# Moving half of the modulation's partial sums to GpSimd, and the substitution of the small diagonal blocks to VectorE

## The chip, the cores and the metric

The kernel runs on one core of one Trainium2 chip. The metric is the device time of one launch in microseconds. The times are those of repeated launches of the same program; the profile is one further execution, recorded by the hardware profiler.

## The reference

One decoder block for 256 tokens of width 2048, in float32. A vector `c` gives six modulation vectors of 2048 elements each; the normalised input is scaled and shifted by the first two, one wide projection feeds a recurrent branch (RWKV-7) and a windowed attention branch, both are gated, merged and added to `x`, and a squared-ReLU MLP follows.

```python
c_act = jax.nn.silu(c)
mod = c_act @ w_ada[l] + b_ada[l]                      # 2048 x 12288
sh1, sc1, gt1, sh2, sc2, gt2 = [m[:, None, :] for m in jnp.split(mod, 6, axis=-1)]
h = rms_norm(x, norm1_gain[l]) * (1.0 + sc1) + sh1
p = h @ w_in[l] + b_in[l]
...
y_rwkv = rwkv7_branch(p_rwkv, ...)                     # a scan over 256 tokens, 16 heads of 64
y_attn = sliding_window_sink_attention(q, k, v, attn_sinks[l])
merged = g_rwkv * (y_rwkv @ w_branch_rwkv[l]) + g_attn * (y_attn @ w_branch_attn[l])
x = x + gt1 * (merged @ w_out[l])
h = rms_norm(x, norm2_gain[l]) * (1.0 + sc2) + sh2
x = x + gt2 * (jnp.square(jax.nn.relu(h @ w_up[l])) @ w_down[l])
return rms_norm(x, final_gain)
```

## The kernel before

**Weights.** Every large product goes through `feed` or `rows_product`. Both take the weight in tiles of 128 x 1024 floats (512 KB): a DMA from the SyncE queue into a tile `raw`, a cast on ScalarE to a rounded copy `whi` (L278), a subtraction on VectorE that leaves the remainder `wlo` (L279), and then 24 matmuls of 256 columns (or 12 of 512) on TensorE (L301, L323). `whi` and `wlo` have four buffers each, `raw` has seven.

**The modulation** is a product of one row with a 2048 x 12288 matrix. It is cut in segments of 2048 columns (`seg`, six of them) and those in pieces: `ada_tile` (L141) loads 128 x 2 x 512 floats (512 KB) into a buffer of the same seven `raw` buffers, and `ada_dve` (L211) multiplies each half by one column of `cact` and adds it into `acc` (L221 for the first half of the first piece, L223 for the others). Eight pieces make 512 columns; `ada_sum` (L186) then sums `acc` over the partitions with four matmuls against a column of ones (L190) and adds the bias on VectorE (L192, L194). The first 512 columns of segments 0 and 1 are done by TensorE (`ada_pe`).

**Order.** Three lists of generators, `bg` (modulation), `att` (attention) and `rw` (recurrence), stand beside the weight stream. After each weight tile `pulse(0.5)` advances every list by its rate; for `bg` the rate counts double, so that `rate["bg"]` is the number of steps per weight tile. What is written in this order is then laid out by a scheduler, engine by engine; each engine and the SyncE queue run their own list strictly in order.

**Stages.** The projection runs in four parts of four blocks of the contraction (`SL`), 16 weight tiles each. While parts 0, 1 and 2 run, `modulated(1)` to `modulated(3)` (L377) compute the 512 columns of segments 1 and 0 that the next part's input needs, 16 pieces each at 1.5 steps per tile; `finish(bg)` closes each part. After the parts come the rest of the projection (gates, keys; tiles of 256 columns x 4 blocks), the attention branch's product, the recurrent branch's product, the output product and the MLP. Segments 2, 4 and 3 (`ada_vec`, L227; 32 pieces each) run under these at `RATE_BG` 0.9, then 0.3 and 0.4 steps per tile; segment 5 runs under the MLP at 0.2.

**The recurrence** runs in two passes of four of the eight head pairs. Each pass has `prep` (which clears one column of `eP` on GpSimd at L510 before VectorE's scan at L529 reads it), `inverse16` (L613), `levels` and `chains`. `inverse16` loads the 128 diagonal 16 x 16 blocks, one a partition, from a DRAM scratch tile (L616), inverts them by 15 steps of a multiply and an add on GpSimd (L624, L626; 15 to 64 elements a partition), copies the transposed blocks (L628), and sends both through another DRAM tile back into `dds` (L627, L629, L634), which `levels` reads on TensorE.

## Time and profile before

| | us |
|---|---|
| time, median of 3 runs | 1545.87 (1545.2 to 1548.84) |
| time of the profiled execution | 1552.83 |
| span in its profile | 1551.1 |
| TensorE busy | 1488.3 |
| VectorE busy | 1099.2 |
| ScalarE busy | 721.6 |
| GpSimd busy | 40.5 |

The span is the profiled execution from its first to its last instruction; 1.7 us of its own time lie around it, and its own time lies 7.0 us above the median of the runs. Matmuls overlap in the pipeline and their ends are modelled, so TensorE's busy share is no measure of how close it is to its peak. Waits are put down to the releaser that came last by the profile. A row of a group of instructions gives the line, the engine, the operation, the tiles written and read, their shape and the count, then the busy time in us and the mean of one in ns, and behind the second bar the idle time before them and what ended it.

### The profile page before, as it was taken

The numbers are of one execution on the slowest core, as the hardware profiler recorded it, in microseconds if no ns is written. First come the engines' busy times: TensorE is split into PE (matmuls) and PEld (weight loads), VectorE is DVE, ScalarE is ACT, GpSimd is POOL, SyncE is SP. The second block draws the span as 40 slices with busy tenths as digits, with TensorE's granted clock in tenths as the row PEclk, the third lists the DMA queues.
The fourth block names the chain that finished last, engine by engine and source line by source line (L and its number), as shares of the span: only waits on it lengthen the run. The fifth ranks groups of instructions, "written<-read, shape, count | busy, mean of one in ns | idle before, by whom it ended". The sixth has DMA issues, their size and how long they took to land.

```text
span 1551.1 us, 30141 instructions
## 1 busy us (share of the span) xinstructions
PE 1488.3 (96%) x12122; PEld 1366.5 (88%) x12122; DVE 1099.2 (71%) x1784; ACT 721.6 (47%) x1107; POOL 40.5 (3%) x97
## 2 busy tenths in 40 slices
PE   5899999999999989999899999999999999999997
PEld 2898998999898989899789998989899898989985
DVE  1979979978689947768679765666666665555576
ACT  3354377656364424444456544434344443444443
POOL 2000000030000030000000000000000000000000
PEclk9899999999999999999999999999999999999998
DMA  9999977779898768878775777777776776666662
GB/s 331 334 317 318 353 236 230 245 191 327 244 288 287 233 188 287 266 252 301 247 234 167 237 226 237 217 224 231 222 232 213 233 229 204 189 190 190 196 185 82
DMA packets 297100, 372.80 MB, mean 240 GB/s; under 512 B 40912, under 2 KB 198384, under 8 KB 296320
## 3 DMA queue, kind: packets, MB, share of 16 engines
q1 hardware_dynamic: 296448, 370.72, 75.3%
q8 instruction: 95, 1.56, 0.4%
q0 software_dynamic: 512, 0.15, 0.1%
q14 instruction: 45, 0.37, 0.1%
HBM read 357.96 MB, written 12.86 MB: 239 GB/s over the span
## 4 chain that ended last, share of the span: by engine, by line
PE 77%; DMA 8%; DVE 8%; issue 2%; POOL 2%; ACT 2%; SPq 1%; DVEq 0%; POOLq 0%; ACTq 0%
PE mm L301 34%; PE mm L323 14%; PE ax L323 14%; PE ax L301 7%; DMA ada<-in_w_ada_dram 5%; DVE acc L223 2%; DVE wlo L279 2%; DMA raw<-in_w_in_dram 1%; PE ax L190 1%; POOL p L626 1%; PE ax L688 1%; POOL rs L624 1%; PE ax L482 1%; PE ax L571 1%; ACT whi L278 1%
## 5 line engine op out<-in xcount | busy, mean ns | idle before, releaser
L278 ACT CAST whi<-raw 128x1024 fp32r<-128x1024 f32 x458 | 478.5, 1048 | 605.8 <-PE ax L323 219.7
L279 DVE TENSOR_TENSOR wlo<-raw,whi 128x1024 fp32r<-128x1024 f32 x458 | 557.2, 1220 | 241.0 <-ACT whi L278 237.1
L301 PE MATMUL mm<-h,whi 128*128 128x256 f32 (+1 forms) x3296 | 433.4, 282 | 3.4 <-ACT whi L278 3.4
L301 PEld LDWEIGHTS mm<-h,whi 128*128 128x128 f32 (+1 forms) x3296 | 403.7, 188 | 10.2 <-ACT whi L278 3.8
L223 DVE SCALAR_TENSOR_TENSOR acc<-ada,cact,acc 128x512 f32<-128x512 f32 x330 | 247.1, 749 | 88.4 <-DMA ada<-in_w_ada_dram 84.0
L301 PE MATMUL mm<-h,wlo 128*128 128x256 f32 (+1 forms) x1648 | 232.7, 282 | 0.0
L301 PEld LDWEIGHTS mm<-h,wlo 128*128 128x128 f32 (+1 forms) x1648 | 210.8, 190 | 0.4 <-DVE wlo L279 0.2
L323 PE MATMUL mm<-whi,u 128*128 128x512 f32 x512 | 137.2, 390 | 0.0
L323 PE MATMUL ax<-whi,u 128*128 128x512 f32 x512 | 136.9, 389 | 0.0
L301 PE MATMUL ax<-h,whi 128*128 128x256 f32 x768 | 106.8, 287 | 9.3 <-DVE p L974 4.7
L323 PEld LDWEIGHTS ax<-whi,u 128*128 128x128 f32 x512 | 96.1, 188 | 20.0
L323 PEld LDWEIGHTS mm<-whi,u 128*128 128x128 f32 x512 | 95.5, 188 | 19.3
L301 PEld LDWEIGHTS ax<-h,whi 128*128 128x128 f32 x768 | 98.0, 194 | 11.7 <-ACT whi L278 5.1
L323 PE MATMUL mm<-wlo,u 128*128 128x512 f32 x256 | 78.8, 389 | 0.0
L323 PE MATMUL ax<-wlo,u 128*128 128x512 f32 x256 | 78.8, 389 | 0.0
L301 PE MATMUL ax<-h,wlo 128*128 128x256 f32 x384 | 57.8, 283 | 0.0
L323 PEld LDWEIGHTS mm<-wlo,u 128*128 128x128 f32 x256 | 48.1, 188 | 10.0
L323 PEld LDWEIGHTS ax<-wlo,u 128*128 128x128 f32 x256 | 48.1, 188 | 10.0
L301 PEld LDWEIGHTS ax<-h,wlo 128*128 128x128 f32 x384 | 51.3, 193 | 0.0
L301 PE MATMUL mm<-a,whi 128*128 128x256 f32 x256 | 37.9, 299 | 0.0
L323 PE MATMUL mm<-whi,m 128*128 128x512 f32 x128 | 36.3, 401 | 0.0
L323 PE MATMUL ax<-whi,m 128*128 128x512 f32 x128 | 36.1, 403 | 0.0
(345 smaller groups left out, 1493.2 us busy)
## 6 DMA issues: line engine op xcount, KB each, us to landing
ada<-in_w_ada_dram SPq DMA_DIRECT2D x192, 512.0 KB, 5.9
raw<-in_w_up_dram SPq DMA_DIRECT2D x128, 512.0 KB, 4.1
raw<-in_w_down_dram SPq DMA_DIRECT2D x128, 512.0 KB, 4.1
raw<-in_w_in_dram SPq DMA_DIRECT2D x72, 512.0 KB, 6.0
raw<-in_w_in_dram SPq DMA_DIRECT2D x128, 256.0 KB, 5.7
raw<-in_w_out_dram SPq DMA_DIRECT2D x32, 512.0 KB, 5.3
raw<-in_w_branch_attn_dram SPq DMA_DIRECT2D x16, 512.0 KB, 5.9
raw<-in_w_branch_rwkv_dram SPq DMA_DIRECT2D x16, 512.0 KB, 5.2
```

The lines of the kernel that those rows point to most:

```text
L190: TE.matmul(ps[:, j:j + 1], lhsT=acc[:, j * P:(j + 1) * P], rhs=ones[:, 0:1], start=True, stop=True)
L223: V.scalar_tensor_tensor(o, in0=t[:, a, :], scalar=ck, in1=o, op0=ALU.mult, op1=ALU.add)
L278: S.copy(hi[:], raw[:])
L279: V.tensor_tensor(lo[:], raw[:], hi[:].bitcast(F32), op=ALU.subtract)
L301: TE.matmul(ps[0:m, j * tw:(j + 1) * tw], lhsT=wt[:, kk, o:o + m], rhs=xx(k), start=(k == begin and xx is xh and wt is hi and j == 0), sto ...
L323: TE.matmul(pss[tb][:], lhsT=uu(k)[:, sl], rhs=wt[:, kk, :], start=(first and k == 0), stop=(final and k == kblocks - 1))
L482: TE.matmul(out[hs, :], lhsT=src[hs, chunk(c)], rhs=ident[hs, hs], start=True, stop=True)
L571: TE.matmul(pT[hs, o:o + P], lhsT=src[hs, chunk(c)], rhs=ar[hs, i, c].rearrange("p a b -> p (a b)"), start=True, stop=True)
L624: G.tensor_tensor(t_, a16[:, s, m:16].unsqueeze(2).broadcast_to([P, n, m]), x16[:, 0, s:s + 1, 0:m].broadcast_to([P, n, m]), op=ALU.mult)
L626: G.tensor_tensor(x16[:, 0, m:16, 0:m], x16[:, 0, m:16, 0:m], t_, op=ALU.add)
L688: TE.matmul(ps[hs, j, i, part, :], lhsT=lhs(j, i, hs), rhs=rhs(j, i, hs), start=(first and j == 0 and i == 0), stop=True, skip_group_check ...
```

## The change

Four edits. `ada_pool` is new: it does a piece on GpSimd, with one multiplication of the whole 128 x 1024 tile by two columns of `cact` (in place), and two additions of 512 columns into its own `acc` (one for the first piece); it has one empty step before its `ada_sum`. `turns` runs several generators a step each in turn. `modulated(1)` to `modulated(3)` and `ada_vec` now give segment 0 (or every second group of 512 columns) to `ada_pool` and segment 1 (or the other groups) to `ada_dve`. `inverse16` moves its 30 operations and the copy from GpSimd to VectorE and takes one of the empty steps behind it to before it. `RATE_BG[0]` goes from 0.9 to 1.0.

```diff
-RATE_BG = (0.9, 0.3, 0.4, 0.2)
+RATE_BG = (1.0, 0.3, 0.4, 0.2)
...
+    def ada_pool(seg, k0, n, dst, gain):
+
+        acc = wp.tile([P, 512], F32, tag="acc", bufs=NACC, name=nm("acc"))
+        o = acc[:, 0:n * P]
+        m = 8 // n
+        for q in range(2 * n):
+            t = ada_tile(seg, k0, n, q)
+            G.tensor_tensor(t[:], t[:], cact[:, m * q:m * q + m].unsqueeze(2).broadcast_to([P, m, n * P]), op=ALU.mult)
+            if q == 0:
+                G.tensor_tensor(o, t[:, 0, :], t[:, 1, :], op=ALU.add)
+            else:
+                for a in range(m):
+                    G.tensor_tensor(o, t[:, a, :], o, op=ALU.add)
+            yield
+        yield
+        ada_sum(acc, n, dst, k0, seg, gain)
+
+    def turns(gens):
...
     def ada_vec(seg, dst, gain=None):
-        for k0 in range(0, KC, 4):
-            yield from ada_dve(seg, k0, 4, dst, gain)
+        for k0 in range(0, KC, 8):
+            yield from turns([ada_dve(seg, k0, 4, dst, gain), ada_pool(seg, k0 + 4, 4, dst, gain)])
...
+            yield from turns([ada_pool(0, k0, n, sh1, None), ada_dve(1, k0, n, sc1, colC[:, 96:96 + KC])])
...
+        yield
         for s in range(15):
...
-            G.tensor_tensor(t_, a16[:, s, m:16].unsqueeze(2).broadcast_to([P, n, m]),
+            V.tensor_tensor(t_, a16[:, s, m:16].unsqueeze(2).broadcast_to([P, n, m]),
...
-            G.tensor_tensor(x16[:, 0, m:16, 0:m], x16[:, 0, m:16, 0:m], t_, op=ALU.add)
+            V.tensor_tensor(x16[:, 0, m:16, 0:m], x16[:, 0, m:16, 0:m], t_, op=ALU.add)
...
-        G.tensor_copy(x16[:, 1], x16[:, 0].rearrange("p a b -> p b a"))
+        V.tensor_copy(x16[:, 1], x16[:, 0].rearrange("p a b -> p b a"))
...
-        for _ in range(5):
+        for _ in range(4):
             yield
```

How the instructions stand now (line numbers of the kernel changed: L308 is the subtraction that was L279, L1006 the eviction that was L974).

**Part 1 of the projection, VectorE before.** `acc_1173` collects a piece of the modulation, `p_44` a projection's sum.

```order
L223 SCALAR_TENSOR_TENSOR acc_1173<-ada_1250,cact,acc_1173 128x512
L974 TENSOR_TENSOR p_44_235<-ax_1178,p_44_235 128x512
L223 SCALAR_TENSOR_TENSOR acc_1173<-ada_1250,cact,acc_1173 128x512
L974 TENSOR_TENSOR p_44_235<-ax_1179,p_44_235 128x512
L279 TENSOR_TENSOR wlo_1262<-raw_1258,whi_1261 128x1024
L223 SCALAR_TENSOR_TENSOR acc_1173<-ada_1289,cact,acc_1173 128x512 x2
L279 TENSOR_TENSOR wlo_1297<-raw_1293,whi_1296 128x1024
L223 SCALAR_TENSOR_TENSOR acc_1173<-ada_1324,cact,acc_1173 128x512 x2
L223 SCALAR_TENSOR_TENSOR acc_1173<-ada_1328,cact,acc_1173 128x512
```

The same place on VectorE now:

```order
L223 SCALAR_TENSOR_TENSOR acc_1021<-ada_1255,cact,acc_1021 128x512
L1006 TENSOR_TENSOR p_44_235<-ax_1182,p_44_235 128x512
L223 SCALAR_TENSOR_TENSOR acc_1021<-ada_1255,cact,acc_1021 128x512
L1006 TENSOR_TENSOR p_44_235<-ax_1183,p_44_235 128x512
L308 TENSOR_TENSOR wlo_1267<-raw_1263,whi_1266 128x1024
L308 TENSOR_TENSOR wlo_1303<-raw_1299,whi_1302 128x1024
L223 SCALAR_TENSOR_TENSOR acc_1021<-ada_1330,cact,acc_1021 128x512 x2
```

And on GpSimd in the same part, where no instruction stood before:

```order
L234 TENSOR_TENSOR ada_986<-ada_986,cact 128x1024
L236 TENSOR_TENSOR acc_985<-ada_986 128x512
L234 TENSOR_TENSOR ada_1026<-ada_1026,cact 128x1024
L239 TENSOR_TENSOR acc_985<-ada_1026,acc_985 128x512 x2
L234 TENSOR_TENSOR ada_1097<-ada_1097,cact 128x1024
L239 TENSOR_TENSOR acc_985<-ada_1097,acc_985 128x512 x2
```

Between two weight tiles VectorE has half as many pieces of the modulation; GpSimd has eight multiplications and fifteen additions in each of three parts.

**GpSimd from the first heads on, before.** `kd` holds the attention's keys, `p_...` are the `eP` tiles that `prep` clears, `rs` and `p_522` belong to `inverse16`.

```order
L910 COPY kd<-a_50_249 64x256 x4
L510 MEMSET p_358_2634 128x4
L510 MEMSET p_367_2651 128x4
L510 MEMSET p_440_3229 128x4
L510 MEMSET p_444_3241 128x4
```

And now:

```order
L942 COPY kd<-a_50_249 64x256 x4
L541 MEMSET p_358_2655 128x4
L234 TENSOR_TENSOR ada_3056<-ada_3056,cact 128x1024
L236 TENSOR_TENSOR acc_3055<-ada_3056 128x512
L541 MEMSET p_367_2672 128x4
L234 TENSOR_TENSOR ada_3251<-ada_3251,cact 128x1024
L239 TENSOR_TENSOR acc_3055<-ada_3251,acc_3055 128x512 x2
L234 TENSOR_TENSOR ada_3417<-ada_3417,cact 128x1024
```

The small clears that VectorE's scans wait for now stand behind pieces of the modulation; the `inverse16` rows that followed them are gone from GpSimd.

**The second `inverse16`, now on VectorE.** `rs_7031` and `p_914` are its product and its blocks, `lg_7028` the loaded blocks.

```order
L308 TENSOR_TENSOR wlo_7149<-raw_7146,whi_7148 128x1024
L656 TENSOR_TENSOR rs_7031<-lg_7028,p_914_7030 128x15
L308 TENSOR_TENSOR wlo_7187<-raw_7184,whi_7186 128x1024
L658 TENSOR_TENSOR p_914_7030<-p_914_7030,rs_7031 128x15
L656 TENSOR_TENSOR rs_7031<-lg_7028,p_914_7030 128x28
L658 TENSOR_TENSOR p_914_7030<-p_914_7030,rs_7031 128x14x2
L656 TENSOR_TENSOR rs_7031<-lg_7028,p_914_7030 128x39
L658 TENSOR_TENSOR p_914_7030<-p_914_7030,rs_7031 128x13x3
```

These rows stood on GpSimd without others between them; now they stand among the subtractions for the weight stream, which follow in the same queue.

## Rows read from the trace of the kernel before

**Rows 1.** The page: busy time and share of the span of each engine.

```profile
PE 1488.3 (96%) x12122; PEld 1366.5 (88%) x12122; DVE 1099.2 (71%) x1784; ACT 721.6 (47%) x1107; POOL 40.5 (3%) x97
```

**Rows 2.** Busy time by stage; the first row names the columns.

```profile
core 0: us, PE busy (x) PEld busy (x) DVE busy (x) ACT busy (x) POOL busy (x), PEclk, DMA share, GB/s
38.00:189.00 151.00, 137.02 (x1102) 134.51 (x1101) 134.52 (x181) 62.02 (x77) 0.00 (x0) 0.95 0.99 331
247.00:655.00 408.00, 391.07 (x4750) 364.63 (x4749) 322.47 (x744) 198.81 (x415) 28.98 (x68) 0.98 0.82 255
857.00:1551.00 694.00, 683.46 (x4385) 623.08 (x4383) 434.40 (x485) 297.52 (x334) 0.00 (x0) 0.99 0.67 208
```

**Rows 3.** VectorE's groups between 38 and 189 us.

```profile
L223 DVE SCALAR_TENSOR_TENSOR acc<-ada,cact,acc 128x512 f32<-128x512 f32 x90 | 67.3, 749 | 1.7
L279 DVE TENSOR_TENSOR wlo<-raw,whi 128x1024 fp32r<-128x1024 f32 x45 | 54.4, 1220 | 5.3 <-ACT whi L278 5.1 <-DMA raw<-in_w_in_dram 0.2
L390 DVE TENSOR_TENSOR h<-ar,h 128x256 fp32r<-128x256 f32 x8 | 3.1, 422 | 0.9 <-ACT h L389 0.8
L221 DVE TENSOR_SCALAR acc<-ada,cact 128x512 f32<-128x512 f32 x6 | 2.9, 483 | 0.1
```

**Rows 4.** Who waited for whom, 38 to 189 us: us in total, times, longest.

```profile
ACT whi L278 <- DMA raw<-in_w_in_dram: 46.2, 23, 4.7
ACT whi L278 <- DVE acc L223: 13.9, 4, 5.5
```

**Rows 5.** Who waited for whom over the span, SyncE's DMA queue.

```profile
SPq L290 <- DVE wlo L279: 278.9, 158, 6.9
```

**Rows 6.** GpSimd's operations, 321 to 339 us; last, a clear at the start.

```profile
L626 POOL TENSOR_TENSOR p<-p,rs 128x15 f32<-128x15 f32 x2 | 0.5, 227 | 0.2
L624 POOL TENSOR_TENSOR rs<-lg,p 128x15 f32<-128x15 f32 x2 | 0.4, 216 | 42.7 <-DMA lg<-scr 42.6
L626 POOL TENSOR_TENSOR p<-p,rs 128x64 f32<-128x64 f32 x1 | 0.3, 318 | 0.1
L624 POOL TENSOR_TENSOR rs<-lg,p 128x64 f32<-128x64 f32 x1 | 0.3, 295 | 0.1
...
L608 POOL MEMSET a<- 128x520 f32 x1 | 0.6, 551 | 0.0
```

**Rows 7.** GpSimd and VectorE in order of time: start us, us, what; at 551.7 us.

```profile
551.97 1.15 POOL L626 TENSOR_TENSOR p<-p,rs 128x48 f32<-128x48 f32 x1
...
551.68 1.29 DVE L279 TENSOR_TENSOR wlo<-raw,whi 128x1024 fp32r<-128x1024 f32 x1
```

**Rows 8.** The same view at 337.8 us.

```profile
337.81 0.64 POOL L628 COPY p<-p 128x256 f32<-128x256 f32 x1
337.88 1.65 DVE L279 TENSOR_TENSOR wlo<-raw,whi 128x1024 fp32r<-128x1024 f32 x1 [1.82 <-ACT whi L278]
```

**Rows 9.** VectorE's groups between 247 and 655 us.

```profile
L223 DVE SCALAR_TENSOR_TENSOR acc<-ada,cact,acc 128x512 f32<-128x512 f32 x148 | 110.7, 748 | 41.1 <-DMA ada<-in_w_ada_dram 39.5
L279 DVE TENSOR_TENSOR wlo<-raw,whi 128x1024 fp32r<-128x1024 f32 x87 | 106.4, 1229 | 20.3 <-ACT whi L278 19.3 <-PE mm L301 0.8
L221 DVE TENSOR_SCALAR acc<-ada,cact 128x512 f32<-128x512 f32 x9 | 4.3, 483 | 2.2 <-DMA ada<-in_w_ada_dram 2.2
L360 DVE TENSOR_TENSOR rd<-rd 128x4 f32<-128x4 f32 x22 | 3.2, 156 | 0.0
```

**Rows 10.** The chain that ended last, 247 to 655 us: shares by engine and line.

```profile
by line: PE mm L301 21.9%; DMA ada<-in_w_ada_dram 14.0%; issue 6.5%; DVE wlo L279 6.3%; DVE acc L223 6.2%; POOL p L626 3.7%; PE ax L688 3.6%; POOL rs L624 3.1%; PE ax L571 2.4%; PE ax L482 2.3%; DMA raw<-in_w_in_dram 2.0%; DMA lw<-in_rwkv_w
```

**Rows 11.** In order of time: the starts of both substitutions, and VectorE then.

```profile
321.45 0.21 POOL L624 TENSOR_TENSOR rs<-lg,p 128x15 f32<-128x15 f32 x1 [42.63 <-DMA lg<-scr]
...
322.65 0.16 DVE L840 TENSOR_SCALAR m<-m 128x4 f32<-128x4 f32 x1
...
548.48 0.58 POOL L624 TENSOR_TENSOR rs<-lg,p 128x15 f32<-128x15 f32 x1 [42.68 <-DMA lg<-scr]
...
548.90 1.24 DVE L279 TENSOR_TENSOR wlo<-raw,whi 128x1024 fp32r<-128x1024 f32 x1
```

**Rows 12.** Who waited for whom between 857 and 1551 us.

```profile
ACT whi L278 <- PE ax L323: 184.2, 114, 2.6
```

**Rows 13.** The chain over the span in order of time: 384 matmuls of 256 columns.

```profile
1046.79 45.23 PE mm L301 x384
```

More of the change, by code (lines that the diff above doesn't have):

```diff
@@ L225, in ada_dve @@
         ada_sum(acc, n, dst, k0, seg, gain)
+    def ada_pool(seg, k0, n, dst, gain):
[14 more added lines that the diff above has]
+    def turns(gens):
+        gens = list(gens)
+        while gens:
+            for g in list(gens):
+                try:
+                    next(g)
+                except StopIteration:
+                    gens.remove(g)
+                    continue
+                yield
     def ada_vec(seg, dst, gain=None):
-        for k0 in range(0, KC, 4):
-            yield from ada_dve(seg, k0, 4, dst, gain)
+        for k0 in range(0, KC, 8):
+            yield from turns([ada_dve(seg, k0, 4, dst, gain), ada_pool(seg, k0 + 4, 4, dst, gain)])
     def drain(g):
@@ L378, in modulated @@
         k0, n = sum(SL[:part]), SL[part]
-        gemv = ada_pe if part == 0 else ada_dve
-        for seg in (1, 0):
-            yield from gemv(seg, k0, n, *((sc1, colC[:, 96:96 + KC]) if seg else (sh1, None)))
+        if part == 0:
+            for seg in (1, 0):
+                yield from ada_pe(seg, k0, n, *((sc1, colC[:, 96:96 + KC]) if seg else (sh1, None)))
+        else:
+            yield from turns([ada_pool(0, k0, n, sh1, None), ada_dve(1, k0, n, sc1, colC[:, 96:96 + KC])])
         for k in range(k0, k0 + n):
@@ L620, in inverse16 @@
         yield
+        yield
         for s in range(15):
```

## The prediction, made before the changed kernel was run

> **What bounds the kernel now.** I read the page's busy shares first: TensorE is busy 96% of the span and VectorE 71% [rows 1]. An average over stages says little, so the busy time by stage comes next [rows 2]. It shows three kinds of time. From 857 us on, the MLP, TensorE is busy 683 of 694 us and VectorE 434, and ScalarE's cast waits for TensorE to give buffers back, 184.2 us on one of its two lines alone [rows 12]. What VectorE or GpSimd do there is hidden: each weight tile takes 24 matmuls of 45.23/384 = 118 ns, 2.83 us [rows 13], against 1.2 us of subtraction. I call this stage C. From 38 to 189 us (stage A: the three projection parts that have the modulation in the background) VectorE is busy 134.5 of 151 us, 89%, and the DMA engines are busy 0.99 of the time at 331 GB/s [rows 2]; the cast waits for weights 46.2 us and for VectorE 13.9 us [rows 4], and the SyncE queue waits for VectorE before it can refill a buffer [rows 5]. So VectorE and the transfers bound stage A together. From 247 to 655 us (stage B: recurrence, attention and both branch products) VectorE is busy 322 of 408 us, the DMA engines 0.82 [rows 2], and the chain of work there is mixed: TensorE, 14% of waiting for pieces of the modulation to land, and 3.7% + 3.1% of GpSimd's substitution, 28 us [rows 10].
>
> **What leaves VectorE.** A piece costs it two operations of 0.75 us [rows 3], 1.5 us. In stage A half of 48 pieces go: 33.7 us of L223 and 1.5 us of L221, so VectorE's own work falls from 134.5 to 99 us. In stage B there were (148 + 9)/2 = 78 pieces [rows 9]. The weight tiles there number about 88; at 1.0 instead of 0.9 steps a tile, and with two empty steps in each 34, they now carry 88 x 32/34 = 83 pieces, 41 on either engine. That takes 37 x 1.5 = 56 us from VectorE.
>
> **What GpSimd pays for a piece.** No row has a GpSimd operation of that size, so I bound it. Two points of the substitution give a slope: the multiply goes from 216 ns at 15 elements to 295 at 64, 1.6 ns an element; the add from 227 to 318, 1.9 ns [rows 6]. At 1024 elements the multiply is then 0.22 + 1009 x 0.0016 = 1.8 us, and the add of 512 is 0.23 + 497 x 0.0019 = 1.15 us. Eight pieces (8 multiplies, 15 adds) take 14.5 + 17.3 = 32 us on GpSimd, where VectorE needs 12. The low end is the clear, which reads nothing: 551 ns for 520 elements, 1.06 ns each [rows 6], which gives 8 x 1.1 + 15 x 0.54 = 17 us. I take 32, since it comes from the same operation with two inputs.
>
> The Trainium skill, "GPSIMD Engine Reference", section "Performance versus the Vector engine", gives 4497 ns for an add of 2048 floats; as an estimate, half and a quarter of that make 8 x 2.25 + 15 x 1.12 = 35 us for eight pieces. No run here shows that size yet.
>
> **Whether that work lies beside VectorE's.** This decides the case. Two rows show that the two engines hold each other up. An add of 48 elements on GpSimd that started inside a subtraction of VectorE (551.68, 1.29 us) took 1.15 us instead of 0.3 and ended 0.15 us after it [rows 7]: GpSimd waited for VectorE's end. And a subtraction that started 0.07 us after a GpSimd copy of 0.64 us took 1.65 us instead of 1.22 [rows 8]: VectorE waited 0.43 us, until 0.14 us before the copy's end. The rows have only short GpSimd operations; I assume that a long one holds VectorE off in the same way, for its length less 0.14 us. Eight pieces then hold VectorE's operations with two SBUF inputs (L223, L279, L390) off for 32 - 23 x 0.14 = 29 us at most.
>
> What the Trainium skill says speaks against the change: "SBUF — State Buffer", section "SBUF: two separate sides", has the port pair that VectorE and GpSimd share as an exclusive lock, taken by whichever starts first and held for the whole instruction, also against a VectorE operation with two SBUF inputs. Rows 7 and 8 agree for operations up to 0.64 us; by this rule the next paragraph's sum holds, and if the 0.43 us seen were the most that one operation can block, the first rival's sum would.
>
> **Stage A.** VectorE's own work 99 us, GpSimd's hold 3 x 29 = 87 us. If the two simply exclude each other, that is 186 us, plus the 16 us that VectorE had idle at the joints of the parts, 202; if GpSimd also runs under the evictions and the joints, what is left is the work that excludes each other: 54.4 + 33.7 + 3.1 + 87 = 178 us. Against 151 us now this is +27 to +51; I take +40. With GpSimd's low end (17 - 3 = 14 us for eight pieces) it is 91 + 42 = 133 us, below the 151 that the transfers need anyway: 0. The transfers leave nothing to gain here: DMA share is 0.99.
>
> **Stage B.** VectorE's own work is 322 - 56 + 62 substitution operations. These I price between its smallest operations, 0.156 us [rows 9], and 0.2 us: 10 to 12 us. That makes 277 us. GpSimd holds 41/8 x 29 = 149 us. VectorE's two-input work (106 of subtractions, 61 of pieces, some 65 of small operations) fills about 230 of 408 us, 57%, so I expect 57% of 149, 85 us, of blocked time; the ends are half of that and all of it, 42 and 149. VectorE goes from 322 to 362 (319 to 426). Off this come half of the 41 us that it waited for pieces to land [rows 9], 21 us, which GpSimd now waits out, and the substitution's 28 us on the chain [rows 10] less its 11 on VectorE, 17 us. Sum: +40 - 21 - 17 = +2, ends -41 and +66. Added waits: the scan on VectorE waits for a clear on GpSimd, which now stands behind pieces, and the subtractions stand behind the scan; eight clears at up to one piece (1.8 + 2.3 = 4.1 us), of which TensorE's lead of up to four tiles hides most: 0 to +33, I take +8. `ada_sum`'s matmuls now wait for GpSimd's sum in TensorE's queue; the empty step gives it one tile: 0 to +10, I take +5. VectorE may also wait for the substitution's blocks to land; they landed at 321.4 and 548.5 us, and VectorE stood at the new place at about 322.6 and just before 548.9 [rows 11]: nothing. Stage B: +15, from -40 to +75.
>
> **Stage C and the rest.** 16 pieces of segment 5 leave VectorE, which waited for TensorE there anyway: 0. If GpSimd's holds came in a row they would be 4 us against a lead of four tiles, 11 us: still 0. Between 655 and 857 us few pieces are left: 0.
>
> **Sum.** +40 + 15 = +55 us on the profiled execution's own time, 1552.8, which gives 1608. That execution lies 7.0 us above the median of the runs, so I state 1601 and round to 1600.
>
> **The rivals.**
> *The blocking is short, and VectorE is relieved* (faster). If a GpSimd operation blocks VectorE by no more than the 0.43 us seen, stage A has 69 x 0.43 = 30 us of it: 99 + 30 + 16 is below 151, so the transfers bound it and it stays. Stage B gets 41/8 x 23 x 0.43 x 0.57 = 29 us of blocking for 45 us less work, and gains the 38 us of waits: 29 - 45 - 38 = -54, or -41 with the added waits. That gives 1492 to 1505; with GpSimd at its low price and full blocking (41/8 x 14 x 0.57 = 41 us) it is -42, with the added waits -29, or near -5 when they are large: 1504 to 1541. It decides where the blocked time of all 65 pieces in A and B falls below what VectorE saves. For it: VectorE is near its bound in stage A and pieces' landing is on the chain. Against it: both rows show waiting until the other's end. Chance 0.17.
> *The losses and gains meet*, within 0.3% of before (1541 to 1550.5; about what a measurement of this kernel can tell from no change): stage A at +30, stage B at -30. 0.06.
> *TensorE starves* (much slower). If stage A feeds a tile every 202/48 = 4.2 us where TensorE needs 2.83, it idles a third of the time. Its granted clock was 0.95 in stage A [rows 2]; if it fell to the lower level, 1.2 GHz, for half of the stage, its 136 us of work would become 204, and the clears and `ada_sum` waits come out at their upper ends (+43). 1650 to 1690. 0.13.
> That the change doesn't do what it says is excluded: GpSimd's queue has the 24 + 64 pieces.
>
> **How the numbers follow.** The forecast, slower by about 55 us (1550.5 to 1650), has 0.64; the rivals 0.17, 0.06 and 0.13. Faster by over 0.3%: 0.17; same 0.06; slower 0.64 + 0.13 = 0.77. The predicted time is the forecast's, 1600. Leaving out the faster rival below 1538 (0.15) and the slow one above 1665 (0.05) gives the range 1538 to 1665.
>
> **What would show it.** VectorE's L308 (subtraction) in stage A at a mean well over 1.22 us, near 2, and L223 over 0.75; GpSimd's multiply near 1.8 us and its add near 1.15 when alone, longer beside VectorE; the stage from the first part to the last fed part longer by 27 to 51 us; no change from the MLP's start on. I am wrong if L308 keeps its 1.22 us while GpSimd works, or if GpSimd's multiply takes about 1.1 us; and wrong in stage B if its length falls although L308 is stretched.

## The result, and the profile after

The changed kernel takes 1666.71 us (median of 4 runs, 1665.03 to 1669.34), the kernel before 1547.36 us beside it (4 runs, 1545.2 to 1549.53): a ratio of 1.0761, 95% interval 1.0729 to 1.0792. It is slower by 119 us. The prediction said slower, at 1600 us with a range up to 1665: the sign was right, the size was less than half of what came.

Three views follow: the page's busy times of the kernel after, then the busy time by stage of before (three rows) and of after (four rows). The stages are cut at the same places of the program: the first row of before is from the attention's first copy to the reload that opens the recurrent branch's product, the next to the start of the MLP's normalisation, the third from there to the end. After has the three fed parts (stage A) ahead of these; before has them in [rows 2]. The columns are those of [rows 2].

```profile
PE 1525.9 (92%) x12122; PEld 1393.9 (84%) x12122; DVE 1201.1 (72%) x1670; ACT 720.3 (43%) x1107; POOL 503.5 (30%) x288
```

```profile
208.00:661.00 453.00, 436.02 (x5126) 408.39 (x5125) 359.99 (x836) 237.94 (x506) 30.79 (x74) 0.98 0.81 251
661.00:829.00 168.00, 163.15 (x1013) 144.26 (x1012) 121.83 (x182) 78.30 (x116) 0.00 (x0) 0.98 0.77 252
829.00:1551.00 722.00, 711.46 (x4619) 651.08 (x4617) 461.95 (x542) 319.20 (x375) 0.00 (x0) 0.99 0.66 206
```

```profile
36.00:225.00 189.00, 153.24 (x1107) 147.71 (x1107) 179.35 (x134) 62.98 (x78) 137.53 (x69) 0.86 0.85 270
244.00:745.00 501.00, 452.35 (x5121) 421.70 (x5121) 412.84 (x810) 234.21 (x497) 215.49 (x130) 0.94 0.73 227
745.00:934.50 189.50, 167.75 (x1018) 146.91 (x1017) 124.06 (x176) 80.53 (x125) 46.81 (x21) 0.94 0.67 221
934.50:1665.80 731.30, 713.21 (x4616) 651.07 (x4614) 464.64 (x508) 319.22 (x375) 94.06 (x46) 0.99 0.63 203
```

From these rows the stages grow like this: up to the attention's start 208 to 244 us (+36; stage A in it 151 to 189, +38), then 453 to 501 (+48), 168 to 189.5 (+21.5), 722 to 731.3 (+9.3). VectorE was to be relieved and is busier: 1201 us against 1099 [rows 1], with 114 instructions fewer.

What VectorE does in stage A now, its groups between 36 and 225 us (after):

```profile
L308 DVE TENSOR_TENSOR wlo<-raw,whi 128x1024 fp32r<-128x1024 f32 x46 | 82.8, 1823 | 0.7 <-DMA raw<-in_w_in_dram 0.7
L223 DVE SCALAR_TENSOR_TENSOR acc<-ada,cact,acc 128x512 f32<-128x512 f32 x45 | 71.8, 1597 | 0.8
L1006 DVE TENSOR_TENSOR p<-ax,p 128x512 f32<-128x512 f32 x8 | 5.2, 680 | 0.4 <-PE ax L330 0.4
L417 DVE TENSOR_SCALAR ar<-ar,sc,sh 128x256 f32<-128x256 f32 x4 | 3.9, 984 | 0.7 <-ACT h L416 0.7
```

Against [rows 3], half as many pieces (45 of L223 instead of 90) take more time than all did (71.8 us instead of 67.3), since one takes 1597 ns instead of 749; the subtraction takes 1823 instead of 1220. Of these rows only L1006, whose one input lies in PSUM (`ax`), kept its length (L974, the same line before, took 685 ns). VectorE is busy 179 of the 189 us: the engine is not short of work, its operations are held. How, in order of time (start us, length, what; after, stage A):

```profile
117.22 1.21 DVE L308 TENSOR_TENSOR wlo<-raw,whi 128x1024 fp32r<-128x1024 f32 x1
117.24 2.94 POOL L234 TENSOR_TENSOR ada<-ada,cact 128x1024 f32<-128x1024 f32 x1 [0.49 <-DMA ada<-in_w_ada_dram]
118.35 4.08 DVE L223 SCALAR_TENSOR_TENSOR acc<-ada,cact,acc 128x512 f32<-128x512 f32 x2
120.26 3.29 POOL L239 TENSOR_TENSOR acc<-ada,acc 128x512 f32<-128x512 f32 x2
122.35 2.28 DVE L308 TENSOR_TENSOR wlo<-raw,whi 128x1024 fp32r<-128x1024 f32 x1
```

The subtraction starts 0.02 us before GpSimd's multiplication and has its normal 1.21 us; the multiplication, 1.89 us when alone (the shortest of the 88), takes 2.94, about the subtraction's rest and its own time. VectorE's next two operations, 0.75 us each alone, take 4.08 us together, to 122.43. So here the two engines alternate, one operation each; [rows 7] and [rows 8] had shown that either can wait for the other, for small ones.

GpSimd's own groups in the same stretch, and what its operations waited for there:

```profile
L239 POOL TENSOR_TENSOR acc<-ada,acc 128x512 f32<-128x512 f32 x42 | 75.1, 1787 | 3.3
L234 POOL TENSOR_TENSOR ada<-ada,cact 128x1024 f32<-128x1024 f32 x24 | 58.0, 2415 | 60.9 <-PE ax L190 23.6 <-DMA ada<-in_w_ada_dram 22.6 <-DVE tt L1006 9.9
```

The second loser is the queue that issues all loads. Its waits for GpSimd over the span (us in total, times, longest; after), and the cast's wait for weights in stage A, which was 46.2 us in [rows 4]:

```profile
SPq L319 <- POOL acc L239: 137.6, 23, 11.8
SPq L358 <- POOL acc L239: 87.3, 10, 10.2
SPq L145 <- POOL acc L239: 30.6, 9, 8.9
```

```profile
ACT whi L307 <- DMA raw<-in_w_in_dram: 81.0, 25, 8.5
```

A piece holds one of the seven `raw` buffers until GpSimd's second addition is through. SyncE issues in order, so a load that needs that buffer stops those behind it.

### The profile page after: what moved, and what is told of

The parts are those of the page before. It is cut to its first block, busy times and chain, and to the rows that moved or that the text cites. A ratio compares the mean times of both kernels' runs of the same rounds, so it can differ in the third digit from the quotient of the medians.

```text
span 1665.8 us, 30276 instructions
## 1 busy us (share of the span) xinstructions
PE 1525.9 (92%) x12122; PEld 1393.9 (84%) x12122; DVE 1201.1 (72%) x1670; ACT 720.3 (43%) x1107; POOL 503.5 (30%) x288
## 5 line engine op out<-in xcount | busy, mean ns | idle before, releaser
L308 DVE TENSOR_TENSOR wlo<-raw,whi 128x1024 fp32r<-128x1024 f32 x458 | 628.7, 1385 | 216.5 <-ACT whi L307 211.7
L234 POOL TENSOR_TENSOR ada<-ada,cact 128x1024 f32<-128x1024 f32 x88 | 208.6, 2370 | 789.0 <-DMA ada<-in_w_ada_dram 482.8
L330 PE MATMUL mm<-h,whi 128*128 128x256 f32 (+1 forms) x3296 | 441.3, 286 | 4.3 <-ACT whi L307 4.3
L330 PEld LDWEIGHTS mm<-h,whi 128*128 128x128 f32 (+1 forms) x3296 | 411.9, 192 | 11.7 <-ACT whi L307 5.3
L223 DVE SCALAR_TENSOR_TENSOR acc<-ada,cact,acc 128x512 f32<-128x512 f32 x165 | 181.6, 1101 | 129.1 <-DMA ada<-in_w_ada_dram 127.1
L239 POOL TENSOR_TENSOR acc<-ada,acc 128x512 f32<-128x512 f32 x154 | 266.4, 1730 | 12.0
L330 PE MATMUL ax<-h,whi 128*128 128x256 f32 x768 | 116.0, 303 | 12.6 <-DVE p L1006 6.8
L330 PEld LDWEIGHTS ax<-h,whi 128*128 128x128 f32 x768 | 107.1, 211 | 15.8 <-issue 7.3
L330 PE MATMUL ax<-h,wlo 128*128 128x256 f32 x384 | 63.0, 300 | 11.1 <-DVE wlo L308 11.1
L330 PEld LDWEIGHTS ax<-h,wlo 128*128 128x128 f32 x384 | 55.3, 207 | 12.3 <-DVE wlo L308 12.3
```

Of the source, the lines that this page charges most:

```text
L223: V.scalar_tensor_tensor(o, in0=t[:, a, :], scalar=ck, in1=o, op0=ALU.mult, op1=ALU.add)
L234: G.tensor_tensor(t[:], t[:], cact[:, m * q:m * q + m].unsqueeze(2).broadcast_to([P, m, n * P]), op=ALU.mult)
L239: G.tensor_tensor(o, t[:, a, :], o, op=ALU.add)
L308: V.tensor_tensor(lo[:], raw[:], hi[:].bitcast(F32), op=ALU.subtract)
L330: TE.matmul(ps[0:m, j * tw:(j + 1) * tw], lhsT=wt[:, kk, o:o + m], rhs=xx(k), start=(k == begin and xx is xh and wt is hi and j == 0), sto ...
```

## The experiments

The theory: GpSimd's operations that read SBUF exclude VectorE's; the loss is that blocked time. Rivals: GpSimd's late release of load buffers (the queue above), the substitution, the added waits, or GpSimd's mere length. Each time below is a median; the ratio with its 95% interval is to runs of the kernel before taken beside it (their medians are 1545.6 to 1551.2). Where a run replaces GpSimd's arithmetic, this is what is taken out of the changed kernel; only what takes its place is shown then.

```diff
-            G.tensor_tensor(t[:], t[:], cact[...].unsqueeze(2).broadcast_to([P, m, n * P]), op=ALU.mult)
-            if q == 0:
-                G.tensor_tensor(o, t[:, 0, :], t[:, 1, :], op=ALU.add)
-            else:
-                for a in range(m):
-                    G.tensor_tensor(o, t[:, a, :], o, op=ALU.add)
```

**The parts of the change.** First the modulation of stage A alone, in the kernel before (`ada_pool` and `turns` added as in the change, `modulated` shared between the engines, the rest untouched):

```diff
-        gemv = ada_pe if part == 0 else ada_dve
-        for seg in (1, 0):
-            yield from gemv(seg, k0, n, *((sc1, colC[:, 96:96 + KC]) if seg else (sh1, None)))
+        if part == 0:
+            for seg in (1, 0):
+                yield from ada_pe(seg, k0, n, *((sc1, colC[:, 96:96 + KC]) if seg else (sh1, None)))
+        else:
+            yield from turns([ada_pool(0, k0, n, sh1, None), ada_dve(1, k0, n, sc1, colC[:, 96:96 + KC])])
```

> The kernel before with only the three projection parts' modulation shared with GpSimd; the later segments, the rate and the substitution as before. If the stages add up, the time is before plus what the profile after lost by its projection parts, 36 us: 1575 to 1590 for both theories; by theory 1 the subtractions there are near 1.8 us.

1588.06 us, 1.0258 (1.0217 to 1.0299): +42. Then the reverse, the whole change with `modulated` as it was before:

> The changed kernel with the three projection parts' modulation back on VectorE; the later segments stay shared. If the stages add up, 1667 less the 42 us that the parts alone cost: 1615 to 1635. If the shared parts' delay was partly made up later: above 1640.

1628.05 us, 1.0508 (1.0477 to 1.0538): +79. The two add up to 121; the change is 119. Then the substitution alone, in the kernel before:

```diff
+        yield
         for s in range(15):
-            G.tensor_tensor(t_, ...)
+            V.tensor_tensor(t_, ...)
-            G.tensor_tensor(x16[:, 0, m:16, 0:m], ...)
+            V.tensor_tensor(x16[:, 0, m:16, 0:m], ...)
...
-        G.tensor_copy(x16[:, 1], x16[:, 0].rearrange("p a b -> p b a"))
+        V.tensor_copy(x16[:, 1], x16[:, 0].rearrange("p a b -> p b a"))
...
-        for _ in range(5):
+        for _ in range(4):
             yield
```

> The kernel before with only the substitution on VectorE (and the empty step moved). By the prediction's step it takes GpSimd's 28 us off the chain for 11 us of VectorE, and by the run with GpSimd's work cut away all gains together are 15 us: 1530 to 1546. A rival: VectorE, in order, waits for the blocks to land and holds the weight stream up: 1550 to 1565.

1545.11 us (10 runs, 1535.25 to 1554.78), 0.9977 (0.9956 to 0.9998). The substitution costs nothing and saves a few us. By its profile stage B is 9 us shorter (453 to 444), but that execution is the shortest of the ten and is already 4 us shorter up to the attention, where nothing was changed, so 9 is the most it can be. So the whole loss is in the modulation. Last, segment 5 (under the MLP) left on VectorE:

```diff
     def ada_vec(seg, dst, gain=None):
+        if seg == 5:
+            for k0 in range(0, KC, 4):
+                yield from ada_dve(seg, k0, 4, dst, gain)
+            return
```

> The changed kernel with segment 5, the one under the MLP, back on VectorE. By the prediction nothing there counts: 1660 to 1670. If GpSimd's reads hold VectorE up there too and TensorE's lead of four tiles does not cover it, the 10 us that the MLP grew come back: 1650 to 1660.

1657.6 us, 1.0713 (1.0689 to 1.0737), and the MLP's stage is back where it was; compare the last row of after above (this kernel, by stage):

```profile
939.00:1661.00 722.00, 711.34 (x4618) 650.92 (x4616) 461.91 (x541) 319.13 (x375) 0.00 (x0) 1.00 0.66 206
```

So the 16 pieces there did cost some 9 us, which were counted at nothing.

**Does GpSimd's mere length do it?** Its reads are replaced by writes of about the same total time:

```diff
+            G.memset(t[:], 0.0)
+            for _ in range(7):
+                G.memset(o, 0.0)
+            G.memset(t[:], 0.0)
```

> The changed kernel with GpSimd's three operations on a piece replaced by clears that only write (one of the 128 x 1024 tile, seven of 512 columns, one of the tile), about 5.8 us a piece as the real ones took in the profile; half of the modulation's sums are left out. The tile is held as long, GpSimd is as busy, but reads nothing. Theory 1 (GpSimd's reads and VectorE's two-input operations exclude each other): subtractions back at 1.22 us, the time within 1530 to 1575. Theory 2 (the tile that GpSimd holds blocks the ring of seven load buffers): 1640 to 1670, the subtractions short and the cast waiting for weights.

1541.34 us, 0.9959 (0.9938 to 0.998). The page's busy times and VectorE's groups in stage A of this kernel (L306 is the subtraction, L415 the one-input scaling that is L417 after):

```profile
PE 1478.3 (96%) x12122; PEld 1360.3 (89%) x12122; DVE 1005.1 (65%) x1670; ACT 722.5 (47%) x1107; POOL 495.5 (32%) x827
...
L306 DVE TENSOR_TENSOR wlo<-raw,whi 128x1024 fp32r<-128x1024 f32 x46 | 55.8, 1222 | 27.3 <-ACT whi L305 24.1 <-PE mm L328 3.0
L223 DVE SCALAR_TENSOR_TENSOR acc<-ada,cact,acc 128x512 f32<-128x512 f32 x45 | 33.7, 749 | 4.4 <-DMA ada<-in_w_ada_dram 3.6
L415 DVE TENSOR_SCALAR ar<-ar,sc,sh 128x256 f32<-128x256 f32 x4 | 2.4, 626 | 0.7 <-ACT h L414 0.7
```

GpSimd is as busy as in the change (495.5 against 503.5 us), and L306 and L223 have their old lengths. The blocking belongs to what GpSimd reads. This run says little of holding buffers, since most of the clears of `o` were placed ahead of the load's landing: a buffer was held for one short and two long clears, about 2.4 us. The Trainium skill, "SBUF — State Buffer", section "SBUF: two separate sides", says that a VectorE operation with two SBUF inputs contends only with a GpSimd operation that reads SBUF. L306 and L223 at their old lengths agree. In the same section the Trainium skill has VectorE operations in a 2-port performance mode contend with GpSimd, without that condition. L415, with one input, took 626 ns where it had 410 before, so pure writes do hold up some operations; whether L415 runs in that mode no run here shows. A longer version, 11 clears instead of 7, drives GpSimd to its own bound:

> The run with clears that only write, made longer: eleven clears of 512 columns instead of seven, about 8 us a piece, as long as GpSimd needed in the run with short operations (707 us of its time for 88 pieces); half of the modulation's sums are left out. VectorE stays free. If the tile that GpSimd holds and its own length cost what the short operations cost: the projection parts near 219 us and the whole above 1640. If only VectorE's waiting costs: 1535 to 1560.

1589.34 us, 1.0257 (1.0235 to 1.028). GpSimd is busy 175 of the 194 us of stage A there and 39 of the 48 us that this run lies above the one before it are in stage A, so GpSimd's 24 pieces themselves set it. The time lies between the two ranges expected: the length alone does cost once GpSimd has no slack left. In the change it is busy 137.5 of 189 us, and has slack.

**What the relief is worth.** GpSimd's work cut to almost nothing:

```diff
+            if q == 0:
+                G.memset(o, 0.0)
+            G.tensor_tensor(o[:, 0:8], t[:, 0, 0:8], t[:, 1, 0:8], op=ALU.add)
```

> The changed kernel with GpSimd's operations on a piece cut to one add of 8 columns; half of the modulation's sums are left out. Neither long holds nor long occupation of a tile: what relieving VectorE of half the pieces and moving the substitution would be worth if GpSimd's work cost nothing. Theory 1 and 2 alike: 1500 to 1545; if it stays above 1600 both are wrong and the cost lies in the substitution or in the new order.

1531.21 us, 0.9894 (0.9859 to 0.9928). That is about the most that the change could have won had GpSimd's work been free: 15 us. By stage (this kernel, A and B):

```profile
36.00:186.00 150.00, 137.92 (x1116) 135.38 (x1116) 104.42 (x137) 63.46 (x78) 13.28 (x26) 0.94 1.01 342
205.00:636.00 431.00, 426.37 (x5122) 401.46 (x5121) 320.37 (x818) 234.57 (x499) 30.82 (x60) 1.00 0.83 263
```

These rows are the base for the blocking. VectorE does the same work here as after, in A 104.4 us instead of 179.4, in B 320.4 instead of 412.8: it is held for 75 and 92 us.

**Shorter operations.** Each GpSimd operation is cut in four by columns, so that VectorE gets its turn sooner:

```diff
+            cq = cact[...].unsqueeze(2).broadcast_to([P, m, P])
+            for i in range(n):
+                u = t[:, :, i * P:(i + 1) * P]
+                G.tensor_tensor(u, u, cq, op=ALU.mult)
+            for a in range(1 if q == 0 else 0, m):
+                for i in range(n):
+                    sl = slice(i * P, (i + 1) * P)
+                    G.tensor_tensor(o[:, sl], t[:, a, sl], t[:, 0, sl] if q == 0 else o[:, sl], op=ALU.add)
```

> The changed kernel with each of GpSimd's operations cut in four columns blocks: the same elements in 4 times as many, shorter operations. If the loss is the total time that GpSimd's reads hold, it stays or grows with the fixed part of an operation, 264 x 0.2 us and more: 1665 to 1740. If it is the length of a single hold in front of a subtraction that matters (short ones slip between): 1590 to 1640.

1730.1 us, 1.1175 (1.1144 to 1.1206). VectorE's and GpSimd's largest groups over the span, and the SyncE queue's largest wait for GpSimd (this kernel):

```profile
L310 DVE TENSOR_TENSOR wlo<-raw,whi 128x1024 fp32r<-128x1024 f32 x458 | 583.8, 1284 | 303.7 <-ACT whi L309 296.1 <-ACT vt L622 2.9 <-PE ax L332 2.2
...
L241 POOL TENSOR_TENSOR acc<-ada,acc 128x128 f32<-128x128 f32 x616 | 375.4, 644 | 0.0
L237 POOL TENSOR_TENSOR ada<-ada,cact 128x256 f32<-128x256 f32 x352 | 305.6, 897 | 672.2 <-DMA ada<-in_w_ada_dram 314.9 <-DVE wlo L310 102.0 <-DMA raw<-in_w_up_dram 93.4
...
SPq L321 <- POOL acc L241: 257.9, 45, 9.9
```

VectorE is indeed held less (the subtraction 1284 ns over the span, 1385 in the change). But GpSimd has 12 instructions a piece instead of three and is busy 717 us instead of 503.5. At the shortest of each kind (603 ns and 442 ns here, 1887 and 1261 in the change) its operations would take 504 us instead of 374; the rest, which I read as waiting for VectorE, grew as well, from about 118 to 206 us. Half of the operations wait for almost nothing (medians 616 and 459 ns), others for long (up to 6.4 us). And the load queue waits for GpSimd 258 us on one line. Blocking works both ways.

**Reads or late buffers?** Here GpSimd's reads are of its own sum, so that the load buffer is free after a short first read:

```diff
+            if q == 0:
+                G.memset(o, 0.0)
+            G.tensor_tensor(o[:, 0:8], t[:, 0, 0:8], t[:, 1, 0:8], op=ALU.add)
+            for w in (512, 512, 512, 256):
+                G.tensor_tensor(o[:, 0:w], o[:, 0:w], o[:, 0:w], op=ALU.mult)
```

> The changed kernel with GpSimd's operations turned to its own sum tile: after a short add of 8 columns from the loaded tile, which frees the load buffer at once, three multiplies of 512 and one of 256 columns read and write the sum tile, some 4.4 us a piece as the real ones alone; half of the modulation's sums are left out. It reads as long but holds no load buffer. Theory 1 (reads hold VectorE up, nothing else is needed): 1625 to 1670, subtractions as in the changed kernel. If the loss needs the held buffer too: 1550 to 1610.

1592.53 us, 1.0274 (1.0254 to 1.0294): 61 us over the tiny operations. The same with one more read of the load buffer as the last step, which holds it to the end:

```diff
+            G.tensor_tensor(o[:, 0:8], t[:, 0, 0:8], o[:, 0:8], op=ALU.add)
```

> The run with reads of GpSimd's own sum tile, plus one more add of 8 columns from the loaded tile at the end, so that the load buffer is held for as long as GpSimd works; half of the modulation's sums are left out. If the rest of the loss is the held buffer (the ring of seven waits while the reads and VectorE exclude each other): 1650 to 1700. If it is the reads of the loaded tile itself: 1595 to 1615.

1645.4 us, 1.064 (1.0578 to 1.0702): another 53. To tell the read from the hold, the last step becomes a read of `o` alone:

> The other half: the same additional read of 8 columns, but of GpSimd's own sum and not of the load buffer, so that the buffer is free early (sums left out as before). If holding is the price: 1590 to 1605. If one more read is: 1635 to 1650.

1602.98 us, 1.033 (1.0297 to 1.0363). So one more read is 10 us and the hold 42, though VectorE is busy less with the hold (1109.3 us, against 1133.4 with the one more read). A third form, in which the last step clears 8 columns of the buffer, took 1588.9 us, 1.025 (1.0229 to 1.0272):

> As the run with reads and hold, but the last instruction on a piece, which holds the load buffer until GpSimd is through, clears 8 columns of it instead of reading them (the sums of half of the modulation are left out). If the 53 us between reads alone (1592) and reads with hold (1645) are the price of holding the load buffer: 1630 to 1650 again. If they are the price of one more read by GpSimd a piece: 1590 to 1600.

It decides nothing: the clear was laid out after the first of the four reads, so the buffer wasn't held to the end.

**The ring or the queue?** GpSimd's pieces in two buffers of their own (the rest keeps five), first with the change's arithmetic, then with the tiny one as a control:

```diff
-RAWB = 7
+RAWB = 5
...
+            t = ada_tile(seg, k0, n, q, "rawp", 2)
```

> The changed kernel with two load buffers of their own for GpSimd's pieces and five instead of seven for the rest. GpSimd's work is the same. Theory 1: 1640 to 1680, subtractions as long as before. Theory 2: the tiles of the weights no longer wait behind GpSimd's: 1560 to 1620, above all in the stages after 745 us.

> Control for the run with GpSimd's own two load buffers: the same five and two buffers, with GpSimd's operations cut to one add of 8 columns (half of the modulation's sums are left out). If five buffers for the rest cost nothing, 1525 to 1540, as with a ring of seven, and the own ring truly saved nothing. If the smaller ring costs much, above 1580, and then the own ring did save what it cost.

1660.53 us, 1.073 (1.0674 to 1.0786), and 1530.89 us, 0.9875 (0.9823 to 0.9927). Five buffers cost nothing, and two separate ones bring next to nothing on the whole; the loads still stand in one queue. By stage they bring more. This is the run with GpSimd's own two buffers and its arithmetic, from the recurrent branch's product to the MLP's normalisation:

```profile
749.30:921.20 171.90, 159.80 (x975) 139.02 (x972) 136.50 (x164) 79.00 (x121) 45.26 (x23) 0.97 0.73 241
```

After had 189.5 us there, with 50 us of waits of the SyncE queue for GpSimd; 171.9 is among what the kernels without GpSimd's long reads take (163 to 172). The stretch up to the attention is 6 us longer than in after (250.1 against 243.7), for a reason that no run shows. So the loads of GpSimd's pieces go to GpSimd's own queue, one piece ahead, again with both kinds of arithmetic:

```diff
...
+        nxt = ada_tile(seg, k0, n, 0, "rawp", 2, G)
         for q in range(2 * n):
-            t = ada_tile(seg, k0, n, q, "rawp", 2)
+            t = nxt
+            if q + 1 < 2 * n:
+                nxt = ada_tile(seg, k0, n, q + 1, "rawp", 2, G)
```

> GpSimd's pieces go into two buffers of their own and are loaded by GpSimd's own DMA queue, one piece ahead, so that the SyncE queue no longer waits for GpSimd (five raw buffers instead of seven stay for the rest; the arithmetic is that of the change). Theory, that GpSimd's late release does its harm by holding up the in-order load queue: the SyncE queue's waits for acc (about 255 us in the change, some 60 with the two own buffers alone) go to zero, and what is left is the exclusion of the operations: near the 1592 us of the reads without the hold, 1580 to 1615. Rival, that it is the exclusion itself, VectorE and GpSimd in turns, whatever the queue: 1640 to 1665, as with the two own buffers on the SyncE queue (1660). Slower than that would mean that GpSimd's own issues cost it time: its busy time and its idle time at the issues would show it.

> The same buffers and the same queue, with GpSimd's work on a piece cut to one addition of 8 columns (the sums of half of the modulation are left out). A control for the run before: if the loads from GpSimd's queue cost nothing by themselves, 1525 to 1540 us, as with the two own buffers on the SyncE queue (1531); above 1550, the queue itself is dear, and the run before has to be read against this one.

1735.78 us, 1.1237 (1.1203 to 1.1271), and 1578.77 us, 1.0224 (1.0192 to 1.0255). No wait of the SyncE queue for GpSimd's pieces is left, and the kernel is slower. The control says that GpSimd's issues are dear by themselves (+48 over the control on the SyncE queue), but the arithmetic adds 157 us on top, more than the 135.5 in the change (1666.7 less 1531.2). By then I held that GpSimd's late release does its harm through the order of the load queue; as the cause of the whole loss that theory fell. What grew instead is in the page's busy times of the two kernels (first the arithmetic of the change, then the control):

```profile
PE 1540.8 (89%) x12122; PEld 1404.8 (81%) x12122; DVE 1258.6 (73%) x1670; ACT 720.1 (42%) x1107; POOL 528.0 (30%) x376
```

```profile
PE 1495.1 (95%) x12122; PEld 1370.7 (87%) x12122; DVE 996.2 (63%) x1670; ACT 721.0 (46%) x1107; POOL 121.0 (8%) x222
```

VectorE is held 262 us, against 205 in the change (1201.1 less the 995.8 of the tiny operations). With GpSimd's queue freed, the same arithmetic held VectorE more. The last run asks the same for the reads of the sum with the hold:

> Reads and hold as in the run that gave 1645, but GpSimd's pieces in two buffers of their own and loaded by GpSimd's own queue (sums left out as before). Its control with tiny operations took 1579. If the hold costs because GpSimd's late release stops the SyncE queue, only the price of the reads comes on top here, 61 us: 1630 to 1650. If it costs in another way, the full 114 us come on top: 1680 to 1700.

1632.4 us, 1.0556 (1.0493 to 1.062): 54 over its control, instead of 114. There the hold did cost through the SyncE queue, and freeing the queue gave it back; GpSimd's issues took most of it away again (1632 against 1645 us).

**Put together, by stage.** The loss has two prices, and the stages pay them differently. In stage A and in stage B the exclusion is enough for a loss of that size. With GpSimd's own queue, where no wait of the SyncE queue for its pieces is left, the change's arithmetic costs 43 us up to the attention (268.8 against 225.7 of its control) and 86 us from there to the recurrent branch's product; in the change it is 38 and 71 us over the run with tiny operations. The second stretch in the two kernels with GpSimd's own queue (the arithmetic of the change, then the control):

```profile
268.80:811.60 542.80, 460.75 (x5161) 430.05 (x5161) 446.42 (x820) 236.16 (x502) 240.77 (x173) 0.91 0.71 212
225.70:682.70 457.00, 435.32 (x5133) 408.49 (x5132) 322.09 (x821) 236.01 (x503) 55.20 (x102) 0.97 0.81 250
```

In the MLP it is the other way round. The stage from the MLP's normalisation to the end takes 721.6 us in before (722 above, cut at a round figure), with tiny operations and with reads of GpSimd's own sum, and 17.5 us more as soon as the same reads hold the load buffer. These are the run with one more read and the run with the hold:

```profile
871.30:1592.90 721.60, 711.00 (x4615) 650.67 (x4614) 462.90 (x507) 319.44 (x375) 108.17 (x97) 1.00 0.67 206
905.40:1644.50 739.10, 714.31 (x4615) 651.52 (x4613) 450.39 (x507) 319.15 (x375) 104.00 (x97) 0.99 0.62 201
```

VectorE is held more in the first of them (462.9 us busy, 440.0 with tiny operations) and nothing is lost; what costs there is the buffer that comes back late. Of the 21.5 us in the stage ahead of it the own ring gave back some 18, so most of that is the buffer too. How much the held buffer adds in stage B of the change isn't shown: with the short reads the hold made that stretch longer (461.5 to 482.5 us), with the change's arithmetic the own ring left it as it was (501.2 to 499.3). Not shown either is whether a buffer held as long without any read would cost the same, and why VectorE was held 57 us longer once GpSimd's loads no longer waited in SyncE's queue. More buffers for the sums or the loads were not tried.

**A better version.** Of all that computes the whole block, the substitution alone (1545.11 us, 0.9977) is the only one not slower than the kernel before; its gain is 0.3 to 6.8 us, the interval's ends, too little to build on.

## Why the prediction was right and wrong

**GpSimd's price: right.** Forecast 1.8 us for the multiplication and 1.15 for the addition when alone; the shortest measured are 1.887 and 1.261 us, so eight pieces take 34 us, not 32. The Trainium skill, "GPSIMD Engine Reference", section "Performance versus the Vector engine", gave 35 by estimate, nearer by luck: its 2.25 us is 19% high for the one and its 1.12 us 11% low for the other.

**Whether it lies beside VectorE's work: right.** In stage A the two exclude each other for whole operations. The rival of the short blocking (0.43 us each) is out, by L223's 1597 ns in stage A.

**Stage A: right.** Forecast +40, from +27 to +51; measured +38 by the stage's own rows (151 to 189), +36 up to the attention, and +42 for this edit alone. VectorE's own work fell to 104 us (forecast 99) and it was held for 75 (forecast 87), so two small misses cancel: 179 us of VectorE, where the forecast's sum had 186. GpSimd's operations, priced at their shortest, are 24 x 1.887 + 45 x 1.261 = 102 us in that stretch; three quarters of that hold VectorE.

**Stage B: the terms for VectorE were right, and the gains were not.** Forecast 45 us of own work gone and 85 us blocked; the rows show 39.6 (359.99 to 320.37) and 92.5 (320.37 to 412.84). The step that failed is the next one: "Off this come half of the 41 us that it waited for pieces to land ... and the substitution's 28 us on the chain ... less its 11". With 45, 21 and 17 I took 83 us off (for 247 to 655 us; the rows here are a little wider, 208 to 661). The run with tiny operations has all three, and its stage B is 453 - 431 = 22 us shorter (17 in the run with five and two buffers), of which the substitution makes 9 at most. These gains overlap. There was little more to win: TensorE is busy 426 of the 431 us there, 436 of 453 before. That VectorE's spared work falls into time in which it would have waited anyway is my reading; no run takes the first two gains apart. The blocking costs 70 us of length (431 to 501) where I had 85 and 13 for added waits. So the stage is -22 + 70 = +48 instead of -83 + 98 = +15. (The stated upper end, +75, was added up wrongly: +66, +33 and +10 make +109.) VectorE's waits for pieces did go, but GpSimd and the cast wait in its place; in stage B of after:

```profile
POOL ada L234 <- DMA ada<-in_w_ada_dram: 83.5, 17, 10.7
...
ACT whi L307 <- DMA raw<-in_w_in_dram: 36.9, 18, 9.6
ACT whi L307 <- DMA raw<-in_w_branch_attn_dram: 21.1, 9, 7.0
```

**Stage C and 655 to 857: wrong, +9 and +21.5 instead of 0** (here the last two rows of each kernel, cut at 661 and 829 us in before). "If GpSimd's holds came in a row they would be 4 us against a lead of four tiles, 11 us: still 0", and "few pieces are left". The sum priced the time that GpSimd holds VectorE. It put at nothing the time that GpSimd, itself held by VectorE, holds a load buffer. The sign "no change from the MLP's start on" failed with it. A piece takes 4.4 us at the shortest lengths, from the start of its multiplication to the end of its second addition; in the MLP of after the median is 6.4 us. The longest multiplication, in the stage before the MLP, in order of time (after):

```profile
828.18 7.64 POOL L234 TENSOR_TENSOR ada<-ada,cact 128x1024 f32<-128x1024 f32 x1 [9.49 <-DMA ada<-in_w_ada_dram]
828.31 1.22 DVE L266 COPY wide<-gtc 128x2048 f32<-128x2048 f32 x1
```

This multiplication takes 7.64 us (the median of all 88 is 2.17), behind a copy and four subtractions that VectorE ran back to back. With its two additions it keeps its load buffer for over 11 us. In the MLP the SyncE queue waited up to 11.8 us for a single release, and 82.1 + 56.5 us in all on two lines:

```profile
SPq L319 <- POOL acc L239: 82.1, 8, 11.8
SPq L358 <- POOL acc L239: 56.5, 6, 10.1
```

The longest of these is as long as the whole lead. That the buffer is the price there, and not the hold on VectorE, is shown by the stages above: 721.6 us with the reads, 739.1 with the reads and the hold; and 171.9 us with the own ring in the stage before, instead of 189.5.

**Added waits and the substitution.** No wait for a clear or for the substitution's blocks of the size allowed for (8 us) is in the waits of after. The operations of the substitution take 0.16 to 0.23 us on VectorE when nothing holds them (priced at 0.156 to 0.2).

**The sum.** From the spans: 36 + 48 + 21.5 + 9 = 115 us (1665.8 less 1551.1), forecast 55. Of the 60 missing, B is 33, the stretch 655 to 857 is 21.5, C is 9, and A was 4 too high. The rival of the starving TensorE had 1650 to 1690, where the time came out, but not by its mechanism: it wanted stage A at about +53 and the clock at its lower level for half of it. The granted clock fell from 0.95 to 0.86 there, stage A grew by 36, and the surplus came elsewhere. The time lies 2 us above the range: none of its cases had a loss after 655 us, where 31 us came.

## What to carry to other kernels

Work that reads SBUF on GpSimd was not parallel to VectorE's two-input operations here: price it as if it stood in VectorE's own queue (of 102 us in stage A, 75 did), and VectorE's bursts as if they stood in GpSimd's. Look who holds a shared load buffer meanwhile: an engine that is let in late gives it back late, and an in-order load queue passes that on, even to a stage in which neither engine was the limit. And several gains read off one stage (less work, a wait gone, a chain cut) are not to be added until one run, or the engine that is late next, says how far they overlap.

## What the runs showed that was not expected

- One-input operations of VectorE are held as well: the scaling of 128 x 256 (L417) took 984 ns against 410 before, and 626 beside GpSimd's pure writes (four operations each; 411 with the tiny operations). Operations with an input in PSUM (L1006) kept 680 ns.
- Cutting GpSimd's operations in four made the kernel 63 us slower than the change, though VectorE was held less (1730 against 1667 us).
- Loads issued by GpSimd cost it time of their own: 723 ns for each of the 88, and the kernel 48 us in the control (1578.8 against 1530.9), with almost no arithmetic on GpSimd:

```profile
L145 POOL DMA_DIRECT2D ada<-in_w_ada_dram x88 | 63.6, 723 | 27.2 <-POOL acc L239 24.9 <-issue 1.9 <-DVE p L543 0.3
```
